# SSD decay exponents from cumulative sums sent through DRAM as rows, and halo copies on ScalarE

## The chip, the core and the metric

The kernel runs on one NeuronCore of a Trainium2 chip. The metric is the device time of one execution in microseconds. Before the change the median of three runs is 3411.99 us (3408.57 to 3416.47).

## The reference, cut to what matters

One hybrid encoder layer over two sequences, 2048 and 256 tokens of width 1024, which the kernel lays out as 18 tiles of 128 tokens. RMSNorm, one input projection, multi-head latent attention beside a bidirectional Mamba-2 (SSD) mixer, an output projection, a SwiGLU FFN and a last RMSNorm. The change touches the SSD mixer alone: for each chunk of 128 tokens, each of 8 heads and each direction it needs the matrix of decays

```
a_cs   = cumsum(dt * a)                  # within a chunk of 128, per head
decay  = exp(where(l >= s, a_cs[l] - a_cs[s], -inf))
scores = einsum(C, B) * decay            # then times x * dt
```

The backward direction is the same with the order of the tokens reversed. The kernel needs exp(...) * dt[s] for both directions, adds the two, and multiplies by C.B.

## The kernel before, in words

Everything is in fp32; most products run as three fp32r products of split operands (`mm3`, L112 to L115). No order is written out by hand in the stage that the change touches: a planner orders each engine's instructions from its own costs, in the order of the program where several are ready, and each engine then runs its list in that order. All transfers are issued by SP's queue, in one list.

Stage A (to about 325 us) normalizes and transposes x, projects the latents, queries, keys, values, gates and dt. Its first transfers are x, `w_a`, one piece of `w_z`, then the small constants (`later`, L76), then cosines (L207), x of the next block (L184) and the rest of `w_z`, `w_kv`, `w_q` (L174). The transposed, split x goes to DRAM as `d_hT`, 2 MB for each block of two tiles.

Stage B (about 325 to 747 us) is the SSD mixer. It first turns dt into softplus(dt) (`dts`) and dt * a (`dsplit`), L386 to L411. `decay_sums` (L571) gets all cumulative sums for the states by small matmuls. Then nine blocks of two tiles pass through a software pipeline, the loop at L582: in step b the block b is projected (`proj`, L436: 192 matmuls of 256 columns, whose result goes by ScalarE at L445 into `X`, three buffers), its two halo columns are copied from and to its neighbour (`halo`, L455 and L456 on GpSimd), block b-1 goes through the five-tap convolution (`conv`: the first tap on ScalarE at L467, four on VectorE at L469, SiLU at L471; `Y`, two buffers), and the two chunks of block b-2 are scanned (`turn`, `scan`). In each half step `decays` (L480) makes the matrix `e` of one chunk. The input of block b+1 (`hT`, two buffers, 2 MB) is loaded at L427 when the block two before it has been projected; blocks 0 and 1 are still in SBUF from stage A.

`decays` before: for each direction GpSimd writes three masked copies of 128 x 1024 (L488): the high and the low part of dt * a and dt itself, each column broadcast over 128 tokens and set to zero on one side of the diagonal. Two pairs of fp32r matmuls (L505, L506) with a mask of ones sum the first two along the partitions, which gives the exponents; ScalarE takes exp from PSUM (L507), VectorE multiplies by the masked dt (L508), adds the directions (L510) and, in `scan`, multiplies by C.B (L538).

After stage B attention starts, whose first products also use L113 to L115.

Of the kernel before, what the change touches and what calls it, by code (L numbers as in the profile page):

```python
# [11 lines left out]
F32 = mybir.dt.float32  # L12
# [8 lines left out]
P = 128  # L21
# [13 lines left out]
WA = QL + KVL + ROPE + 2 * SH  # L35
SCALE = QKD ** -0.5
MAGIC = float(0x5F3759DF)


@with_exitstack  # L40
def hymba_kernel(ctx: ExitStack, tc: tile.TileContext, io, seqs, dbg=None):
# [50 lines left out]
    cmr = const.tile([P, 2, P], F32R, name="cmr")  # L92
    later.append(lambda: nc.vector.tensor_copy(cmr[:, 0, :], m_gt))
    later.append(lambda: nc.vector.tensor_copy(cmr[:, 1, :], m_lt))

    dtall = const.tile([P, NT, 16], F32, name="dtall")

# [3 lines left out]
    d_kr = dram.tile([ROPE, 2, T], F32, name="d_kr")  # L101
    d_v = dram.tile([T, NH, P], F32, name="d_v")
    d_z, d_y, d_C, d_sb = ([dram.tile([P, SW if m != "C" else NG * P], F32, name=f"d_{m}{i}") for i in range(NT)] for m in ("z", "y", "C", "sb"))
    d_x2 = [dram.tile([P, D], F32, name=f"d_x2{i}") for i in range(NT)]

    def f(t):
# [258 lines left out]


    dpool = pool(mixer, "decays", 1)
    dfs, dtd, dec, dts, dah, dal = (dpool.tile([P, 2, NT, SH], F32, name=m) for m in ("dfs", "dtd", "dec", "dts", "dah", "dal"))
    dsplit = dpool.tile([P, 2, NT, SH], F32, name="dsplit")

    with ExitStack() as ph:
# [5 lines left out]
        with ExitStack() as inner:  # L377
            sb = pool(inner, "t_sb", 1)

            def tmp(name):  # L380
                return sb.tile([P, NT, 16], F32, name=name)

            def bc(row):
                return row.rearrange("p (o h) -> p o h", o=1).to_broadcast([P, NT, 16])

            av = sb.tile([P, 16], F32, name="av")  # L386
            nc.scalar.activation(av, alog, AF.Exp)
            nc.vector.tensor_scalar(av, av, -1.0, None, op0=ALU.mult)
# [16 lines left out]
            dhr = sb.tile([P, 2, NT, SH], F32R, name="dhr")  # L405
# [3 lines left out]
            nc.vector.tensor_copy(dhr, dsplit)  # L409
            nc.vector.tensor_copy(dah, f(dhr))  # L410
            nc.vector.tensor_tensor(dal, dsplit, dah, op=ALU.subtract)  # L411

        wp2 = pool(ph, "b_w2", 1)
        wx += [wp2.tile([P, 2, KD, P], F32R, name=f"wx{j}") for j in range(4, KD)]
# [35 lines left out]
        def halo(b, j):  # L450
            c = slice(j, j + 2)
            if bl[b][0] in starts:
                nc.gpsimd.memset(X[b][:, c, 0:2], 0.0)
            else:
                nc.gpsimd.tensor_copy(X[b][:, c, 0:2], X[b - 1][:, c, n:n + 2])  # L455
                nc.gpsimd.tensor_copy(X[b - 1][:, c, n + 2:n + 4], X[b][:, c, 2:4])  # L456
            if last(b):
                nc.gpsimd.memset(X[b][:, c, n + 2:n + 4], 0.0)

# [17 lines left out]
        def hb(a, d, c):  # L477
            return a[:, d, c, :].rearrange("p (h o) -> p h o", o=1).to_broadcast([P, SH, SP])

        def decays(c, even):  # L480

            w = []
            for d in range(2):
                sign = 1 - 2 * d

                def masked(dst, a):

                    nc.gpsimd.affine_select(dst, a[:, d, c, :].rearrange("p (h o) -> p h o", o=1).to_broadcast([P, SH, P]), pattern=[[0, SH], [sign, P]], compare_op=ALU.is_ge, fill=0.0, base=0, channel_multiplier=-sign)  # L488

                rh = mp.tile([P, SH, P], F32R, name="rh", tag="rh")  # L490
                rl = sb.tile([P, SH, P], F32R, name="rl", tag="rl", bufs=1)
                dm = sb.tile([P, SH, P], F32, name="dm", tag="dm", bufs=1)
                masked(rh, dah)
                masked(rl, dal)
                masked(dm, dts)
                if d:
                    e = sb.tile([P, SH, P], F32, name="e1", tag="e1", bufs=1)
                elif even:
                    e = sb.tile([P, SH, P], F32, name="e0", tag="e0", bufs=2)
                else:  # L500
                    e = st.tile([P, SH, P], F32, name="e0", tag="rawx")
                for hh in range(2):
                    s = slice(hh * 4, hh * 4 + 4)
                    pd = bank("ta").rearrange("p (h l) -> p h l", h=4)
# [66 lines left out]
        def decay_sums():  # L571
            for d, (m1, m2) in enumerate(((m_le, m_gt), (m_ge, m_lt))):
                for m, dst in ((m1, dfs), (m2, dtd), (m_one, dec)):
                    ps = bank("mb")[:, :NT * SH]
                    nc.tensor.matmul(ps, m, dsplit[:, d].rearrange("p c h -> p (c h)"), start=True, stop=True)
                    nc.scalar.activation(dst[:, d], ps.rearrange("p (c h) -> p c h", h=SH), AF.Exp)
                nc.vector.tensor_tensor(dtd[:, d], dtd[:, d], dts[:, d], op=ALU.mult)


        nb = len(bl)  # L580
        decay = {}
        for b in range(nb + 2):  # L582
# [8 lines left out]
            for u in range(4):  # L591
# [593 lines left out]
def layout(inputs):  # L1185
# [36 lines left out]
    out["c_mats"] = np.stack([k == l, k <= l, k > l, k >= l, k < l, k >= 0 * l], axis=1).astype(np.float32)  # L1222
    inv = (np.float32(10000.0) ** (-np.arange(0, ROPE, 2, dtype=np.float32) / np.float32(ROPE))).astype(np.float32)
    ang = np.arange(s, dtype=np.float32)[:, None] * inv[None, :]
    out["c_rope"] = np.stack([np.cos(ang), np.sin(ang)], axis=1).astype(np.float32)
    return {n: np.ascontiguousarray(v) for n, v in out.items()}

# [19 lines left out]
```

## Time and profile before

| | us |
|---|---|
| median of three runs | 3411.99 |
| profiled execution | 3416.36 |
| its span, first to last instruction | 3414.7 |
| TensorE busy over the span | 3244.2 (95%) |
| VectorE busy | 2456.1 (72%) |
| ScalarE busy | 1698.0 (50%) |
| GpSimd busy | 609.4 (18%) |
| mean granted clock of TensorE | 0.974 of full |

Busy shares are means over stages with different limits; what the change is worth is read from 325 to 747 us. An instruction's time in the profile holds the time for which it was held up while running. PE is TensorE, DVE VectorE, ACT ScalarE, POOL GpSimd, SP the queue that issues transfers. L numbers are lines of the kernel before.

### The profile page before, as it was taken

What the parts mean: (1) busy time and instruction counts of PE and PEld (TensorE: products, weight loads), DVE (VectorE), ACT (ScalarE), POOL (GpSimd) and SP (SyncE); (2) the same over time, 40 slices, a digit from 0 to 9 for tenths busy, and PEclk for the clock granted to TensorE, in tenths of its full rate; (3) what the DMA queues carried; (4) which work ended last, traced back from release to release, by engine and by line L of the source; (5) the groups of instructions that cost most, each with busy time, mean ns of one, the idle gap of its engine ahead of it and who ended that gap; (6) DMA issues with size and microseconds to landing.
All of it is one profiled execution on the core that took longest, in us unless ns stands there. A gap on an engine that the chain in (4) does not pass through costs nothing.

```text
span 3414.7 us, 48534 instructions
## 1 busy us (share of the span) xinstructions
PE 3244.2 (95%) x17817; PEld 2882.8 (84%) x17817; DVE 2456.1 (72%) x4396; ACT 1698.0 (50%) x3518; POOL 609.4 (18%) x597
## 2 busy tenths in 40 slices
PE   8998999879999999999799799999999999999988
PEld 7897988858888888887688699999999998778777
DVE  6445799978888888887854777787778776354566
ACT  5453444437777777777311545455544444222233
POOL 2222577750000000000310000000000000432630
PEclk9999999979999999999899899999999999999999
DMA  6565222231022111200642333333333333755664
GB/s 253 191 227 186 90 81 75 69 83 37 27 54 52 39 40 41 54 17 15 224 139 99 142 115 122 142 118 118 137 141 132 113 119 118 230 185 172 224 212 137
DMA packets 259166, 407.24 MB, mean 119 GB/s; under 512 B 21424, under 2 KB 170608, under 8 KB 256368
## 3 DMA queue, kind: packets, MB, share of 16 engines
q1 hardware_dynamic: 258928, 404.15, 35.5%
q8 instruction: 140, 2.29, 0.3%
q14 instruction: 98, 0.80, 0.1%
HBM read 274.98 MB, written 129.11 MB: 118 GB/s over the span
## 4 chain that ended last, share of the span: by engine, by line
PE 78%; DVE 11%; DMA 3%; POOL 3%; issue 3%; ACT 2%; SPq 0%; POOLq 0%; ACTq 0%; DVEq 0%
PE bank_mb L1005 8%; PE bank_ma L1005 8%; PE bank_ta L1005 8%; PE bank_ma L113 6%; PE bank_ma L115 6%; PE bank_ma L114 6%; PE bank_mb L113 5%; PE bank_mb L115 5%; PE bank_mb L114 5%; DVE Y L469 4%; PE bank_ta L721 4%; PE bank_o L729 3%; PE bank_o L730 3%; DMA rawd<-w_down 2%; PE bank_tb L721 2%
## 5 line engine op out<-in xcount | busy, mean ns | idle before, releaser
L938 DVE TENSOR_TENSOR ws<-rawf,ws 128x512 fp32r<-128x512 f32 x396 | 267.8, 687 | 97.2 <-ACT ws L937 95.3
L937 ACT ACTIVATE ws<-rawf 128x512 fp32r<-128x512 f32 x396 | 241.8, 627 | 171.7 <-PE bank_ta L1005 37.2
L1005 PE MATMUL bank_ma<-U,ws 128*128 128x384 f32 x1584 | 302.8, 338 | 6.4 <-ACT U L937 3.2
L1005 PE MATMUL bank_mb<-U,ws 128*128 128x384 f32 x1584 | 304.2, 336 | 2.8 <-ACT c L1014 2.5
L1005 PE MATMUL bank_ta<-U,ws 128*128 128x384 f32 x1584 | 297.3, 334 | 3.5 <-ACT U L937 3.0
L1005 PEld LDWEIGHTS bank_ma<-U,ws 128*128 128x128 f32 x1584 | 279.0, 190 | 8.0 <-ACT U L937 3.5
L129 DVE TENSOR_TENSOR pT<-bank_ta,pT 128x512 fp32r<-128x512 f32 (+1 forms) x352 | 239.6, 681 | 63.2 <-ACT pT L128 54.6
L1005 PEld LDWEIGHTS bank_mb<-U,ws 128*128 128x128 f32 x1584 | 277.4, 189 | 5.1 <-ACT c L1014 4.1
L1005 PEld LDWEIGHTS bank_ta<-U,ws 128*128 128x128 f32 x1584 | 276.7, 188 | 4.5 <-ACT U L937 3.3
L128 ACT ACTIVATE pT<-bank_ta 128x512 fp32r<-128x512 f32 (+1 forms) x352 | 209.1, 595 | 116.7 <-PE bank_ta L721 116.2
L1118 POOL TENSOR_TENSOR rawd<-rawd 128x512 f32<-128x512 f32 x33 | 51.5, 1559 | 1189.0 <-DMA rawd<-w_down 1188.6
L729 PE MATMUL bank_o<-pT,v 128*128 128x512 f32 x528 | 248.7, 471 | 1.9 <-ACT ot L736 1.9
L469 DVE SCALAR_TENSOR_TENSOR Y<-X,cw,Y 128x256 f32<-128x256 f32 x288 | 218.5, 815 | 22.9 <-POOL X L456 15.4
L679 DVE TENSOR_REDUCE mx<-bank_ma 128x1 f32<-128x512 f32 (+1 forms) x261 | 177.0, 678 | 50.1 <-PE bank_ma L115 49.5
L721 PE MATMUL bank_ta<-ident,pr 128*128 128x128 f32 x1388 | 210.6, 273 | 2.0 <-DVE pT L129 2.0
L721 PEld LDWEIGHTS bank_ta<-ident,pr 128*128 128x128 f32 x1388 | 170.5, 140 | 48.7 <-DVE pT L129 8.0
L730 PE MATMUL bank_o<-pT,v 128*128 128x512 f32 x528 | 206.2, 391 | 0.0
L1134 ACT ACTIVATE as<-rawa 128x1408 fp32r<-128x1408 f32 x63 | 86.7, 1378 | 225.6 <-PE bank_ma L115 108.6
L688 ACT ACTIVATE pr<-bank_mb,mx 128x512 f32<-128x512 f32 (+1 forms) x261 | 181.4, 695 | 7.9 <-DVE mx L679 4.8
L688 ACT ACTIVATE pr<-bank_ma,mx 128x512 f32<-128x512 f32 (+1 forms) x261 | 179.1, 686 | 6.4 <-DVE mx L707 5.5
L679 DVE TENSOR_REDUCE mx<-bank_mb 128x1 f32<-128x512 f32 (+1 forms) x261 | 176.9, 678 | 7.0 <-PE bank_mb L115 3.7
L752 POOL TENSOR_TENSOR mla<-lo,ri 128x256 f32<-128x256 f32 (+1 forms) x40 | 22.8, 570 | 855.6 <-DVE lo L751 842.5
(399 smaller groups left out, 8584.9 us busy)
## 6 DMA issues: line engine op xcount, KB each, us to landing
rawf<-w_gu SPq DMA_DIRECT2D x66, 1024.0 KB, 5.8
rawa<-d_A SPq DMA_DIRECT2D x63, 704.0 KB, 5.2
rawd<-w_down SPq DMA_DIRECT2D x154, 256.0 KB, 4.9
d_A<-c SPq DMA_DIRECT2D x132, 192.0 KB, 1.9
d_A<-s SPq DMA_DIRECT2D x99, 192.0 KB, 1.9
o<-d_x SPq DMA_DIRECT2D x32, 512.0 KB, 4.8
d_hT<-hT SPq DMA_DIRECT2D x7, 2048.0 KB, 12.9
hT<-d_hT SPq DMA_DIRECT2D x7, 2048.0 KB, 7.9
```

Source lines behind the costliest of these rows:

```text
L113: nc.tensor.matmul(ps, wh, xh, start=start, stop=False)
L114: nc.tensor.matmul(ps, wh, xl, start=False, stop=False)
L115: nc.tensor.matmul(ps, wl, xh, start=False, stop=stop)
L469: nc.vector.scalar_tensor_tensor(y[:, j, :], x[:, j, t:t + n], cw[:, j, t:t + 1], y[:, j, :], op0=ALU.mult, op1=ALU.add)
L679: nc.vector.tensor_reduce(mx[:, j:j + 1], ps[:, :m * P], axis=AX.X, op=ALU.max, negate=nch == 1)
L688: nc.scalar.activation(e[:, :m * P], ps[:, :m * P], AF.Exp, bias=bias, accum_out=rs[:, i, j:j + 1])
L721: nc.tensor.transpose(ps[:, i * P:(i + 1) * P], pr[i, kt // 4][:, kt % 4 * P:(kt % 4 + 1) * P], ident)
L729: nc.tensor.matmul(po[0][:, :n], v[:, s0 + kt, :], pT[:, 0, :n], start=kt == 0, stop=False)
L730: nc.tensor.matmul(po[0][:, :n], v[:, s0 + kt, :], pT[:, 1, :n], start=False, stop=kt == sn - 1)
L937: nc.scalar.activation(dst[:, 0], src, AF.Copy)
L938: nc.vector.tensor_tensor(dst[:, 1], src, f(dst)[:, 0], op=ALU.subtract)
L1005: nc.tensor.matmul(ps[:, :W], w[:, a, k, :], x[:, b, k, :], start=k + n == 0 and not more, stop=k == HK - 1 and n == 2, skip_group_check=more)
```

## The change: what it does

The masked copies go. Instead the exponents of all chunks are made once and sent through DRAM as rows, and each chunk loads its rows.

Once, at the end of step 0: dt * a is split on a fixed grid into `coarse` and `fine`, `off` is ln(dt); `decay_sums` takes the cumulative sums of `coarse` and `fine` by four more small matmuls, and `off` becomes ln(dt) minus the fine sum. `cum_rows` transposes the three arrays (nine transposes), splits each into two fp32r parts (tile `part`, which shares the two buffers of `Y`) and writes them to `d_cum` and `d_off` with 144 transfers, all on SP. `d_cum` holds a block-diagonal arrangement whose other entries must be zero, so the whole of it, 36 x 32768 numbers (4.72 MB), is copied from an input of zeros beforehand, as the last of the constants in `later`.

For each chunk: `load_rows`, eight transfers (four for each direction), fills the rows 0-15, 16-31 of two halves of `r` (64 x 1024) and `o` (64 x 128); the other rows are constants. There is one `r` and one `o` for each direction, loaded for chunk c+1 after the products of chunk c. `decays` then is, for each half, one fp32r product of `o` and `r` with 64 rows, which gives the difference of cumulative sums plus ln(dt), and one of the identity with a mask of -2^100, and exp. The product by the masked dt (L508) is gone.

The two halo copies go from GpSimd to ScalarE.

```diff
+    later.append(lambda: nc.sync.dma_start(d_cum.rearrange("g a q x -> g (a q x)"), io["c_zero"]))
...
+            nc.vector.tensor_scalar(coarse, dsplit, GRID, None, op0=ALU.add)
+            nc.vector.tensor_scalar(coarse, coarse, -GRID, None, op0=ALU.add)
+            nc.vector.tensor_tensor(fine, dsplit, coarse, op=ALU.subtract)
+            nc.vector.tensor_scalar(off, dts, 1e-37, None, op0=ALU.max)
+            nc.scalar.activation(off, off, AF.Ln)
...
-                nc.gpsimd.tensor_copy(X[b][:, c, 0:2], X[b - 1][:, c, n:n + 2])
-                nc.gpsimd.tensor_copy(X[b - 1][:, c, n + 2:n + 4], X[b][:, c, 2:4])
+                nc.scalar.activation(X[b][:, c, 0:2], X[b - 1][:, c, n:n + 2], AF.Copy)
+                nc.scalar.activation(X[b - 1][:, c, n + 2:n + 4], X[b][:, c, 2:4], AF.Copy)
...
+        def load_rows(c):
+            for d in range(2):
+                r, o = fix[d]
+                for a in range(2):
+                    nc.sync.dma_start(f(r)[a * 32:a * 32 + 16], d_cum[d * NT + c, a].rearrange("q (h x) -> (q h) x", h=SH).rearrange("k (h l) -> k h l", h=SH))
+                    nc.sync.dma_start(f(o)[a * 32 + 16:a * 32 + 32], d_off[d * NT + c, a].rearrange("q h l -> (q h) l"))
...
-                masked(rh, dah)
-                masked(rl, dal)
-                masked(dm, dts)
...
-                    nc.tensor.matmul(pd, cmr[:, d, :], rh[:, s, :], start=True, stop=False)
-                    nc.tensor.matmul(pd, cmr[:, d, :], rl[:, s, :], start=False, stop=True)
+                    nc.tensor.matmul(pd, o, r[:, s, :], start=True, stop=False)
+                    nc.tensor.matmul(pd, identr, never[:, d:d + 1, :].to_broadcast([P, 4, P]), start=False, stop=True)
                     nc.scalar.activation(e[:, s, :], pd, AF.Exp)
-                nc.vector.tensor_tensor(e, e, dm, op=ALU.mult)
...
+        def cum_rows():
+            G3 = 12
+            for src, a, to in ((coarse, 0, "both"), (fine, 1, "cum"), (off, 1, "off")):
+                flat = src.rearrange("p d c h -> p (d c h)")
+                ps = bank("mb")[:96, :384]
+                for t in range(3):
+                    nc.tensor.transpose(ps[:, t * P:(t + 1) * P], flat[:, t * 96:(t + 1) * 96], ident)
+                part = sb.tile([96, 2, 3, P], F32R, name="part", tag="Y")
+                flatp = part.rearrange("p q t l -> p q (t l)")
+                nc.scalar.activation(flatp[:, 0], ps, AF.Copy)
+                nc.vector.tensor_tensor(flatp[:, 1], ps, f(flatp)[:, 0], op=ALU.subtract)
+                n, w = SH - 1, (SH + 1) * P
+                for g in range(G3):
+                    p = f(part)[g * SH:(g + 1) * SH]
+                    for q in range(2):
+                        if to != "cum":
+                            nc.sync.dma_start(d_off[g::G3, a, q].rearrange("t h l -> h t l"), p[:, q])
+                        if to != "off":
+                            nc.sync.dma_start(d_cum[g::G3, a, q, :n * w].rearrange("t (h x) -> h t x", h=n)[:, :, :P], p[:n, q])
+                            nc.sync.dma_start(d_cum[g::G3, a, q, n * w:].rearrange("t (h x) -> h t x", h=1), p[n:, q])
...
+                for t in (coarse, fine):
+                    ps = bank("mb")[:, :NT * SH]
+                    nc.tensor.matmul(ps, m1, t[:, d].rearrange("p c h -> p (c h)"), start=True, stop=True)
+                    nc.vector.tensor_copy(t[:, d], ps.rearrange("p (c h) -> p c h", h=SH))
+                nc.vector.tensor_tensor(off[:, d], off[:, d], fine[:, d], op=ALU.subtract)
+            cum_rows()
+            load_rows(bl[0][0])
...
                     decay[c] = decays(c, b % 2 == 0)
+                    if c + 1 < NT:
+                        load_rows(c + 1)
```

## Rows read from the trace of the kernel before

**Rows 1.** The page's part 2: busy tenths of VectorE and GpSimd in 40 equal slices of the span (85.4 us each).

```profile
DVE  6445799978888888887854777787778776354566
POOL 2222577750000000000310000000000000432630
```

**Rows 2.** Busy time by stretch: a steady block of the SSD loop, and the stage's end (columns: the stretch, its length, then busy us with the count of instructions for PE, PEld, DVE, ACT and POOL, granted clock, DMA share, GB/s).

```profile
449.00:493.50 44.50, 39.84 (x286) 37.34 (x285) 41.09 (x47) 18.53 (x30) 33.47 (x31) 0.96 0.21 78
...
670.00:745.00 75.00, 56.62 (x276) 46.64 (x275) 61.55 (x61) 24.61 (x41) 55.80 (x41) 0.77 0.29 79
```

**Rows 3.** What TensorE waited for from 449 to 493.5 us (us in total, times, the longest).

```profile
PE bank_o L567 <- DVE e L538: 3.2, 2, 2.5
PE bank_tb L554 <- DVE ns L558: 1.5, 1, 1.5
```

**Rows 4.** VectorE's groups from 325 to 745 us, shapes kept apart (busy us, mean ns, idle before and its releasers).

```profile
L469 DVE SCALAR_TENSOR_TENSOR Y<-X,cw,Y 128x256 f32<-128x256 f32 x288 | 218.5, 815 | 22.9 <-POOL X L456 15.4 <-ACT Y L467 7.2
L508 DVE TENSOR_TENSOR e<-e,dm 128x1024 f32<-128x1024 f32 x36 | 60.9, 1691 | 14.5 <-ACT e L507 6.5 <-POOL dm L488 4.3 <-POOL rh L488 3.7
L538 DVE TENSOR_TENSOR e<-e,bt 128x1024 f32<-128x1024 f32 x18 | 29.8, 1654 | 0.1
L510 DVE TENSOR_TENSOR e<-e,e 128x1024 f32<-128x1024 f32 x18 | 27.6, 1533 | 0.3
L568 DVE TENSOR_TENSOR yo<-bank_o,yo 128x512 f32<-128x512 f32 x18 | 12.2, 679 | 2.2 <-PE bank_o L567 2.2
```

**Rows 5.** The tile X: the convolution's taps on VectorE (ns, min/median/max).

```profile
L469 DVE SCALAR_TENSOR_TENSOR Y<-X,cw,Y x288: 468/476/1511, 334.4 to 710.4; 128x256 f32<-128x256 f32 x144
```

**Rows 6.** GpSimd's groups from 325 to 745 us.

```profile
L488 POOL TENSOR_SCALAR_AFFINE_SELECT rh<-dah 128x1024 fp32r<-128x1024 f32 x36 | 52.9, 1470 | 38.7 <-PE bank_ta L505 38.7
L488 POOL TENSOR_SCALAR_AFFINE_SELECT rl<-dal 128x1024 fp32r<-128x1024 f32 x36 | 51.3, 1424 | 0.0
L531 POOL TENSOR_TENSOR xd<-xs,dtd 128x512 f32<-128x512 f32 x36 | 49.9, 1401 | 5.5 <-PE bank_tb L554 5.2 <-POOL ns L557 0.4
L488 POOL TENSOR_SCALAR_AFFINE_SELECT dm<-dts 128x1024 f32<-128x1024 f32 x36 | 47.5, 1320 | 31.4 <-DVE e L508 31.4
L557 POOL TENSOR_TENSOR ns<-ns,dec 128x512 f32<-128x512 f32 x16 | 23.4, 1463 | 8.4 <-DVE ns L558 8.4
L527 POOL TENSOR_TENSOR yo<-xs,rows 128x512 f32<-128x512 f32 x18 | 22.4, 1245 | 1.0 <-ACT xs L518 1.0
L549 POOL TENSOR_TENSOR yo<-yo,to 128x512 f32<-128x512 f32 x16 | 22.0, 1374 | 18.3 <-DVE to L548 18.3
```

**Rows 7.** ScalarE in order of time: evictions of projected block pairs (start us, us). The four evictions of a block end its projection; 372.56 is block 1's last, 677.29 is block 8's last.

```profile
372.56 0.60 ACT L445 ACTIVATE X<-bank_ma 128x512 f32<-128x512 f32 x1 [3.91 <-PE bank_ma L115]
...
677.29 0.60 ACT L445 ACTIVATE X<-bank_ma 128x512 f32<-128x512 f32 x1 [5.10 <-PE bank_ma L115]
```

**Rows 8.** The chain of waits: stage A's last store, and attention's first product.

```profile
324.18 6.31 DMA d_v<-vs
...
747.33 0.79 PE bank_tb L113
```

**Rows 9.** What VectorE waited for from 670 to 750 us (us in total, times, the longest).

```profile
DVE to L548 <- PE bank_tb L546: 6.7, 2, 4.7
...
DVE yo L568 <- PE bank_o L567: 2.2, 1, 2.2
DVE ns L558 <- PE bank_tb L554: 1.4, 1, 1.4
```

**Rows 10.** SP's time for the issue of one transfer (ns, min/median/max): C by head group and queries, which have three levels of addresses, and the plain store of y.

```profile
L473 SPq DMA_DIRECT2D d_C<-Y x18: 518/584/628, 382.1 to 714.2; - x18
L299 SPq DMA_DIRECT2D d_q<-kq x40: 550/584/3165, 66.8 to 321.9; - x40
L569 SPq DMA_DIRECT2D d_y<-yo x18: 319/322/401, 399.8 to 745.2; - x18
```

**Rows 11.** Transfers from 300 to 760 us: median us from issue to landing.

```profile
hT<-d_hT SPq DMA_DIRECT2D x7, 2048.0 KB, 7.9
...
d_q<-kq SPq DMA_DIRECT2D x8, 384.0 KB, 6.4
...
d_C<-Y SPq DMA_DIRECT2D x18, 128.0 KB, 2.2
```

**Rows 12.** The page's part 6: stores of hT over the whole run.

```profile
d_hT<-hT SPq DMA_DIRECT2D x7, 2048.0 KB, 12.9
```

**Rows 13.** SP in order of time at the start: the last constant, the next x, the rest of w_z.

```profile
11.65 0.33 SPq L76 DMA_DIRECT2D rows<-c_rows  x1
...
14.18 1.86 SPq L184 DMA_DIRECT2D xt<-x  x4
...
16.64 2.56 SPq L174 DMA_DIRECT2D raw<-w_z  x3
```

**Rows 14.** What SP's queue waited for in the first 60 us: four of the constants each for one of the four transfers of w_a, issued eight before them.

```profile
SPq L76 <- DMA raw<-w_a: 3.5, 4, 1.0
```

**Rows 15.** TensorE in order of time in stage A: the last gate product of the first block, the first query product.

```profile
37.73 0.39 PE L115 MATMUL bank_mb<-wz,hT 128*128 128x512 f32 x1
...
41.87 0.66 PE L113 MATMUL bank_ma<-wq,lT 128*128 128x384 f32 x1 [0.33 <-ACT lT L131]
```

**Rows 16.** SP in order of time: the loads of blocks 2 and 3 (two transfers, with the wait between them).

```profile
348.86 24.02 SPq L427 DMA_DIRECT2D hT<-d_hT  x2
```

More of the change, by code (lines that the diff above doesn't have):

```diff
@@ L37 @@
 MAGIC = float(0x5F3759DF)
+GRID = 1.5 * 2.0 ** 13
 @with_exitstack
@@ L91, in hymba_kernel @@
     dtb, alog, dskip = rows[:, 0:16], rows[:, 16:32], rows[:, 32:40]
-    cmr = const.tile([P, 2, P], F32R, name="cmr")
-    later.append(lambda: nc.vector.tensor_copy(cmr[:, 0, :], m_gt))
-    later.append(lambda: nc.vector.tensor_copy(cmr[:, 1, :], m_lt))
+    identr = const.tile([P, P], F32R, name="identr")
+    later.append(lambda: nc.vector.tensor_copy(identr, ident))
+    never = const.tile([P, 2, P], F32R, name="never")
+    for d, m in enumerate((m_gt, m_lt)):
+        later.append(lambda d=d, m=m: nc.vector.tensor_scalar(never[:, d], m, -2.0 ** 100, None, op0=ALU.mult))
     dtall = const.tile([P, NT, 16], F32, name="dtall")
@@ L103, in hymba_kernel @@
     d_z, d_y, d_C, d_sb = ([dram.tile([P, SW if m != "C" else NG * P], F32, name=f"d_{m}{i}") for i in range(NT)] for m in ("z", "y", "C", "sb"))
+    d_cum = dram.tile([2 * NT, 2, 2, SH * SH * P], F32, name="d_cum")
+    d_off = dram.tile([2 * NT, 2, 2, SH, P], F32, name="d_off")
+    later.append(lambda: nc.sync.dma_start(d_cum.rearrange("g a q x -> g (a q x)"), io["c_zero"]))
     d_x2 = [dram.tile([P, D], F32, name=f"d_x2{i}") for i in range(NT)]
@@ L367, in hymba_kernel @@
     dpool = pool(mixer, "decays", 1)
-    dfs, dtd, dec, dts, dah, dal = (dpool.tile([P, 2, NT, SH], F32, name=m) for m in ("dfs", "dtd", "dec", "dts", "dah", "dal"))
+    dfs, dtd, dec, dts, coarse, fine, off = (dpool.tile([P, 2, NT, SH], F32, name=m) for m in ("dfs", "dtd", "dec", "dts", "coarse", "fine", "off"))
     dsplit = dpool.tile([P, 2, NT, SH], F32, name="dsplit")
@@ L404, in hymba_kernel @@
             nc.vector.tensor_tensor(da, u, bc(av), op=ALU.mult)
-            dhr = sb.tile([P, 2, NT, SH], F32R, name="dhr")
             for d in range(2):
@@ L408, in hymba_kernel @@
                 nc.vector.tensor_copy(dsplit[:, d], da[:, :, d * SH:(d + 1) * SH])
-            nc.vector.tensor_copy(dhr, dsplit)
-            nc.vector.tensor_copy(dah, f(dhr))
-            nc.vector.tensor_tensor(dal, dsplit, dah, op=ALU.subtract)
+            nc.vector.tensor_scalar(coarse, dsplit, GRID, None, op0=ALU.add)
[3 more added lines that the diff above has]
+            nc.scalar.activation(off, off, AF.Ln)
         wp2 = pool(ph, "b_w2", 1)
@@ L478, in hb @@
             return a[:, d, c, :].rearrange("p (h o) -> p h o", o=1).to_broadcast([P, SH, SP])
+        fix = {}
+        for d in range(2):
+            r = mp.tile([64, SH, P], F32R, name=f"rows{d}")
+            o = mp.tile([64, P], F32R, name=f"offs{d}")
+            raw = sb.tile([64, SH + 1, P], F32, name="rk", tag="Y")
+            nc.sync.dma_start(raw, io["c_rk"].rearrange("k (h l) -> k h l", l=P))
+            nc.vector.tensor_copy(o, raw[:, 0])
+            nc.vector.tensor_copy(r, raw[:, 1:])
+            fix[d] = r, o
+        def load_rows(c):
+            for d in range(2):
+                r, o = fix[d]
+                for a in range(2):
+                    nc.sync.dma_start(f(r)[a * 32:a * 32 + 16], d_cum[d * NT + c, a].rearrange("q (h x) -> (q h) x", h=SH).rearrange("k (h l) -> k h l", h=SH))
+                    nc.sync.dma_start(f(o)[a * 32 + 16:a * 32 + 32], d_off[d * NT + c, a].rearrange("q h l -> (q h) l"))
         def decays(c, even):
@@ L483, in decays @@
             for d in range(2):
[L484 to L492, printed above, removed]
-                masked(rh, dah)
-                masked(rl, dal)
-                masked(dm, dts)
+                r, o = fix[d]
                 if d:
@@ L1224, in layout @@
     ang = np.arange(s, dtype=np.float32)[:, None] * inv[None, :]
+    rk = np.zeros((2, 2, 2, SH, P + SH * P), np.float32)
+    rk[:, 0, :, :, :P] = 1.0
+    rk[:, 1, :, :, P:] = np.repeat(np.eye(SH), P, axis=1)
+    rk[0, 1] *= -1.0
+    rk = rk.reshape(64, -1)
+    out["c_rk"] = rk
+    out["c_zero"] = np.zeros((2 * (a["x_prompt"].shape[1] + a["x_sample"].shape[1]) // P, 4 * SH * SH * P), np.float32)
     out["c_rope"] = np.stack([np.cos(ang), np.sin(ang)], axis=1).astype(np.float32)
```

## The prediction, made before the change was run

> **What bounds the kernel now.** I read the page's slices first: in slices 5 to 9 VectorE is at eight to nine tenths and GpSimd at five to seven, more than anywhere else [rows 1]. Then the stretches: in a steady block of the SSD loop, 44.5 us, VectorE is busy 41.1 and TensorE 39.8 [rows 2]. TensorE's waits there, 4.7 us, all name VectorE [rows 3], so VectorE ends last. Its groups say why: the 288 taps of the convolution take 815 ns in the mean [rows 4] but 476 in the median [rows 5], and the large products 1533 to 1691. Taps run beside GpSimd's masked copies and wait for them inside their own time; L568, which reads PSUM, stays at 679. The stage ends 70.0 us after block 8's last eviction: 677.3 to 747.3 [rows 7, 8], a tail in which VectorE is busy 61.6 of 75 us and TensorE's clock is granted at 0.77 [rows 2].
>
> **The change part by part.**
>
> **1. The steady loop.** GpSimd loses 52.9 + 51.3 + 47.5 = 151.7 us of masked copies and keeps 49.9 + 23.4 + 22.4 + 22.0 = 117.7 [rows 6], 44% of the 269. VectorE loses L508, 60.9 us. I scale what the taps lose to GpSimd (815 - 476 = 339 ns) by that 44%: 149, so a tap takes about 625 ns. For a block: 32 x 0.625 = 20.0; L538 and L510 at 1.4 us each (between 0.97, the taps' ratio of 476 to 815, and their mean of 1.65), twice each, 5.6; six operations from PSUM at 0.68, 4.1. Sum 29.7 against 41.1 now, so VectorE no longer ends last.
> TensorE is late next. Its matmuls stay equal in number and columns (four of 512 columns for each direction, of which half now have 64 rows; the extra ones come once). What it needs for a block: 44.5 less 4.7 of waits, less 4% for the clock at 0.96 [rows 2, 3] (1.8 us): 38.0. I take 39.0 with one us of waits left; the bounds are 38.0 and 42.0 (half the gain kept). Blocks 2 to 8 took 677.3 - 372.6 = 304.7 us [rows 7]; 7 x 39 = 273. **Gain 31.7** (11 to 39).
> The halo copies on ScalarE: it is busy 18.5 of 44.5 us [rows 2]; eight copies of four columns per block cost at most 8 x 0.6, the price of a whole eviction [rows 7], and lie beside its idle time. VectorE's 15.4 us of waits for L456 [rows 4] lie in the gain above. Below nothing: the copy follows the eviction on the same engine.
> `load_rows`, 16 transfers per block at 0.32 to 0.58 us [rows 10], 7 us of SP, and 2 to 3 us to land [rows 11]: they start when chunk c's products have read `r` and have half a block, 20 us, until the next. Queued behind them on SP are d_y, d_C and hT, none needed within 7 us. I cost it at nothing; if they come late each time, a few us per chunk (rival D).
>
> **2. The tail.** L508 goes, and VectorE's backlog of taps with it. What it must do after the last eviction: 8 taps at 0.625 and four scans at 2.8 + 2.0: 24 us; its waits for TensorE's chain stay, 6.7 + 2.2 + 1.4 [rows 9]. That is 35; I take 38. **Gain 32** (20, if 20 us of taps are still behind, to 37).
>
> **3. The burst on SP.** The 144 transfers: coarse 12 x 2 x 3 = 72, fine 48, off 24. Of them 48 take one partition and go at d_y's 0.32 us, 96 have three levels as d_C and queries, 0.58 [rows 10]: 15 + 56 = 71 us of issue. They start at about 337: the space comes free when d_v lands at 330.5 [rows 8], then tables, sums, transposes and splits. The first 120 are ready together and end at about 395, the rest and load_rows(0) at 412. The load of block 2's input stands at 348.9 now [rows 16], when block 0 has been projected; it comes later in the program, so it queues behind 120 to 152 transfers: issued 395 to 412, landed 7.9 us later [rows 11], 403 to 420. TensorE, which now ends block 1 at 372.6 and goes on, has nothing else to run there: the scans need the same rows, and the first convolution a buffer of `Y` that `part` holds until its transfers have landed (395). So block 2 begins at 412 in place of 373. **Loss 39.** Bounds: 19, if the planner puts the hT load in front (then three blocks are projected by 396 and the first rows still land at about 415); 85, if each transfer costs 0.8 us (rival B).
>
> **4. The zero fill.** 4.72 MB, issued behind the last constant at 12 us, ahead of x, w_z, w_kv and w_q [rows 13]. At hT's rate, 2.1 MB in 7.9 us [rows 11], it takes 18 us; at the store's 12.9 us [rows 12], 29. What comes after it is late by that: the queue seems to allow eight transfers outstanding (each of four constants waited for the w_a piece eight before it [rows 14]), so the third w_z piece and all after it wait for its landing. TensorE now ends the first gates at 37.7 and starts on the queries at 41.9 [rows 15]. With the last w_z pieces 18 us later it ends them near 53 and the queries start there: **loss 12** (0, if the planner puts it past the loads; 23 at the slower rate). TensorE is full until 300, so nothing gives it back.
> The rate of a copy from DRAM to DRAM stands in no row. The Trainium skill, page "DMA: Bandwidth & Descriptors", section "Why a DMA increments its semaphore by 16 and not by 1", says that such a transfer runs on the largest number of engines up to 16 that divides its slowest dimension on both sides; 36 rows would make that 12, the fill 18 x 16/12 = 24 us, and the sum about 6 us worse. No run here shows it.
>
> **5. Small things.** Ln on ScalarE, two table loads and the coarse, fine and off arithmetic lie ahead of the burst and are in its 337. The tables `never` and `identr` replace `cmr`, three copies for two.
>
> **The sum.** -31.7 - 32 + 39 + 12 = -12.7. The profiled execution took 3416.4 us, 4.4 above the median: 3403.7 in its terms, 3399 against the median of 3412.0.
>
> **The rivals.**
> **B, slower: the burst lasts.** Each of the 144 waits for a slot among eight outstanding, and stores land in 6.4 us as those of the queries do in this stretch [rows 11]: 6.4 / 8 = 0.8 us each. The hT load then stands behind 120 x 0.8 = 96 us: 337 + 96 + 8 = 441, a loss of 68. Sum -63.7 + 68 + 12 = +16: 3428. It decides once a transfer costs more than 0.65 us (gain 63.7 - 12 = 52 us used up). For it: a list that no one overtakes, DRAM stores of 512-byte pieces, and in-order ScalarE and VectorE lists planned as if they landed sooner. Against: d_C and d_y land in about 2 us.
> **C, faster by much: the burst is out of the way.** The planner puts the hT loads ahead, or an issue costs 0.32 throughout (46 us, to 383, block 2 at 391): a loss of 19, and a fill at nothing to 12. Sum -63.7 + 19 + 6 = -39: 3373. For it: SP is idle most of the stage. Against: the order of the program.
> **D, slower: rows late in every chunk.** One `r` per direction, so TensorE's list stands still if SP is held by a store at its head. Three us in 18 chunks, 54, in place of the loop's gain: sum near +25, 3437. SP's list waited for y, but the rows have 20 us.
> **How the numbers follow.** The forecast 0.45, C 0.20, B 0.25, D 0.10. Within the forecast, sd about 12 us: faster by over 0.2% (7 us, about what a measurement of this kernel can tell from no change) 0.29 of the 0.45, within 0.13, slower 0.03; C all faster; B and D 0.31 slower and 0.04 within. Faster 0.49, same 0.17, slower 0.34. The range takes in C and B and part of D: 3365 to 3438; the forecast's own is 3384 to 3414.
>
> **What would show it.** In the profile after: taps near 0.6 us and no L488 (1); evictions of a block 39 us apart and TensorE's waits for VectorE gone; attention's first product some 38 us after block 8's last eviction (2); 144 short issues on SP from about 337 in a row, the second hT load behind them, TensorE without work between about 373 and 412 (3); w_z landing near 44 us and the first query product near 53 (4). Wrong: taps still at 0.8; TensorE waiting for `r` in each step; block 2 projected before 395, or not until after 430.

## The result, and the profile after

The changed kernel takes 3438.62 us (3438.19 to 3439.08), the kernel before in the same session 3410.28: a ratio of 1.008, 95% interval 1.0063 to 1.0098. It is slower by some 28 us where 13 us faster was forecast.

Both traces can be cut at the same events. First ScalarE's list in the kernel before (start us, us): the first eviction of the SSD stage, block 2's first, and the stage's last operation; [rows 7] has block 1's last and block 8's last.

```profile
329.38 0.59 ACT L445 ACTIVATE X<-bank_ma 128x512 f32<-128x512 f32 x1
...
384.39 0.61 ACT L445 ACTIVATE X<-bank_ma 128x512 f32<-128x512 f32 x1
...
746.68 0.60 ACT L560 ACTIVATE ns<-bank_tb 128x512 f32<-128x512 f32 x1 [6.87 <-PE bank_tb L554]
```

The same five events in the changed kernel, where the eviction is L456 and the state copy L599:

```profile
344.31 0.59 ACT L456 ACTIVATE X<-bank_ma 128x512 f32<-128x512 f32 x1
...
383.71 0.60 ACT L456 ACTIVATE X<-bank_ma 128x512 f32<-128x512 f32 x1 [4.82 <-PE bank_ma L124]
...
447.54 0.60 ACT L456 ACTIVATE X<-bank_ma 128x512 f32<-128x512 f32 x1 [4.32 <-PE bank_ma L124]
...
716.54 0.60 ACT L456 ACTIVATE X<-bank_ma 128x512 f32<-128x512 f32 x1 [5.15 <-PE bank_ma L124]
...
770.21 0.60 ACT L599 ACTIVATE ns<-bank_tb 128x512 f32<-128x512 f32 x1 [5.28 <-PE bank_tb L593]
```

| stretch | before, us | after, us | difference |
|---|---|---|---|
| start to the stage's first eviction | 329.4 | 344.3 | +14.9 |
| to block 1's last eviction | 43.2 | 39.4 | -3.8 |
| to block 2's first eviction | 11.8 | 63.8 | +52.0 |
| to block 8's last eviction | 292.9 | 269.0 | -23.9 |
| to the stage's last operation | 69.4 | 53.7 | -15.7 |
| the rest of the span | 2668.0 | 2666.0 | -2.0 |

The differences add up to +21.5, which is that of the two spans (3436.2 less 3414.7). It is less than 28 because the profiled execution of the kernel before took 3416.36 us, 6 more than the median. Each stretch has its own view.

**The start.** SP in order of time, then what SP's queue waited for from 12 to 45 us, then what TensorE waited for in the first 60 us of the changed kernel (us in total, times, the longest):

```profile
12.97 0.63 SPq L112 DMA_DIRECT2D d_cum<-c_zero  x1
...
29.57 0.33 SPq L216 DMA_DIRECT2D cs<-c_rope  x1
30.01 1.45 SPq L183 DMA_DIRECT2D raw<-w_z  x2
```

```profile
SPq L216 <- DMA d_cum<-c_zero: 12.3, 1, 12.3
```

```profile
PE bank_ta L206 <- DMA raw<-w_z: 12.3, 1, 12.3
```

The eighth transfer behind the fill waits for the fill, and the rest of `w_z` behind that; TensorE's first query product comes at 54.2 us (41.9 in [rows 15]).

**The burst.** SP's first transfer of the burst, its last eleven with the load behind them; then TensorE's longest wait from 345 to 470 us:

```profile
348.56 0.34 SPq L547 DMA_DIRECT2D d_off<-part  x1
...
418.88 3.81 SPq L547 DMA_DIRECT2D d_off<-part  x11
...
426.44 0.37 SPq L438 DMA_DIRECT2D hT<-d_hT  x1
```

```profile
PE bank_ta L523 <- DMA offs<-d_off: 42.3, 1, 42.3
```

The 144 transfers go out back to back for 74 us; the load of block 2's input, at 348.86 us in [rows 16], stands behind all of them and the first eight row loads. ScalarE's list stands too: the first tap of the next convolution waits 28 us for a `Y` slot that `part` holds until its transfers have landed.

```profile
415.33 4.04 ACT L478 ACTIVATE Y<-X,cb,cw 128x256 f32<-128x256 f32 x8 [28.15 <-DMA d_cum<-part]
```

**A steady block.** Busy time in one block from first eviction to first eviction (columns as in [rows 2]), and VectorE's taps over the stage, which answer to [rows 4]:

```profile
492.86:533.53 40.67, 40.67 (x285) 36.66 (x284) 28.90 (x42) 19.52 (x38) 11.83 (x10) 1.00 0.29 100
```

```profile
L480 DVE SCALAR_TENSOR_TENSOR Y<-X,cw,Y 128x256 f32<-128x256 f32 x288 | 166.3, 642 | 59.8 <-ACT X L467 31.4 <-ACT Y L478 28.5
```

VectorE fell from 41.1 to 28.9 us a block, as the forecast had it (29.7). But TensorE is busy the whole 40.67 us and waits for nothing; the forecast gave it 38.0. The reason stands in TensorE's list (start us, us):

```profile
556.34 0.50 PE L523 MATMUL bank_ta<-rows,offs 64*128 64x512 f32 x1
556.77 0.50 PE L524 MATMUL bank_ta<-never,identr 128*128 128x512 f32 x1
557.20 0.49 PE L523 MATMUL bank_ta<-rows,offs 64*128 64x512 f32 x1
557.62 0.50 PE L524 MATMUL bank_ta<-never,identr 128*128 128x512 f32 x1
```

Products of 512 columns at full clock follow each other 0.43 us apart here. They alternate between 64 and 128 rows, which none of the kernel before's decay products did.

**The tail.** Busy time in the last stretch, its first two pieces and the sum over all three:

```profile
716.50:732.50 16.00, 14.18 (x70) 9.97 (x69) 14.83 (x23) 10.61 (x20) 9.14 (x6) 1.00 0.67 158
732.50:752.00 19.50, 19.36 (x58) 12.93 (x59) 13.26 (x21) 7.26 (x9) 5.77 (x4) 0.56 0.10 32
...
sum 53.70, PE 49.04 PEld 35.43 DVE 36.09 ACT 21.95 POOL 26.26; mean PE 16.35 PEld 11.81 DVE 12.03 ACT 7.32 POOL 8.75
```

VectorE is busy 36.1 us, where the forecast's 38 held 24 us of its work and waits for the rest. TensorE is busy 49.0 of 53.7 us, 19.4 of them at a mean granted clock of 0.56, which is mostly the lower of its two levels (1.2 GHz); it fell there after a piece at full clock in which TensorE was busy 14.2 of 16.0 us.

### The profile page after: what moved, and what is told of

It reads as the page before. It is cut to its first block, busy times and chain, and to the rows that moved or that the text cites. A ratio compares the mean times of both kernels' runs of the same rounds, so it can differ in the third digit from the quotient of the medians.

```text
span 3436.2 us, 48810 instructions
## 1 busy us (share of the span) xinstructions
PE 3261.7 (95%) x17834; PEld 2882.3 (84%) x17834; DVE 2343.7 (68%) x4375; ACT 1712.8 (50%) x3580; POOL 425.9 (12%) x433
## 4 chain that ended last, share of the span: by engine, by line
PE 86%; DVE 5%; DMA 2%; ACT 2%; SPq 2%; issue 1%; POOL 1%; POOLq 0%; ACTq 0%; DVEq 0%
PE bank_mb L1053 8%; PE bank_ma L1053 8%; PE bank_ta L1053 8%; PE bank_ma L122 7%; PE bank_ma L124 7%; PE bank_ma L123 7%; PE bank_mb L122 6%; PE bank_mb L124 5%; PE bank_mb L123 5%; PE bank_ta L769 4%; PE bank_o L777 3%; PE bank_o L778 3%; PE bank_tb L769 2%; PE bank_o L1053 2%; PE bank_tb L1053 2%
## 5 line engine op out<-in xcount | busy, mean ns | idle before, releaser
L480 DVE SCALAR_TENSOR_TENSOR Y<-X,cw,Y 128x256 f32<-128x256 f32 x288 | 166.3, 642 | 59.8 <-ACT X L467 31.4
L124 PE MATMUL bank_ma<-hT,wx 128*128 128x256 f32 x576 | 164.8, 286 | 2.7 <-DVE wx L133 2.7
```

Of the source, the lines that this page charges most:

```text
L124: nc.tensor.matmul(ps, wl, xh, start=False, stop=stop)
```

## The experiments

My theory after this reading: three costs lie one behind the other on TensorE's list, the fill (some 14 us), the burst (some 50) and the alternation of row counts (3 us a block). The rivals are in the expectations. Ratios are to the kernel before, run on the same chip; what an edit gains on the changed kernel is the difference of two such ratios, each with its interval.

### The fill, moved and by itself

The first kernel has the fill in the first stage, in its third block; the second is the kernel before with one line more.

```diff
+            if b == 2:
+                nc.sync.dma_start(d_cum[0:1, 0, 0, :8], lats[0][0:1, :8])
+                nc.sync.dma_start(d_cum.rearrange("g a q x -> g (a q x)"), io["c_zero"])
```

```diff
+    later.append(lambda: nc.sync.dma_start(d_cum.rearrange("g a q x -> g (a q x)"), io["c_zero"]))
```

> The same kernel with the zero fill of d_cum issued in the middle of the first stage (behind the first tile of its third block, by a small transfer that it must wait for) in place of 13 us; nothing is left out. Theory: the fill delays the start by what the first eviction of the SSD stage is late, 14.9 us (344.3 against 329.4), and nothing gives it back: first query product near 42 us again, first eviction of the SSD stage near 330, time 3424 (3420 to 3428). Rival 1, the delay was given back before the end of the stage or is another edit's: 3436 to 3441. Rival 2, the fill costs as much wherever it stands, because it takes the DMA engines from the loads of x: 3434 to 3440, with TensorE waiting for x in the third block.

Measured: 3425.69 us, ratio 1.0045 (1.0032 to 1.0057), against 1.008: some 12 us less. The first query product is at 41.6 us, the stage's first eviction at 330.5, and TensorE waits for nothing from 100 to 200 us, where the fill now is. Rival 2 falls.

> The kernel before with the zero fill alone added, at its place behind the constants; nothing else reads d_cum. Theory: plus 12 to 15 us, 3422 to 3426, first query product near 54 us as in the changed kernel. Rival, the fill is hidden or given back: within 4 us of the kernel before, 3406 to 3414.

Measured: 3422.54 us, ratio 1.004 (1.0027 to 1.0052), some 14 us more than before, with the same wait in SP's queue:

```profile
SPq L209 <- DMA d_cum<-c_zero: 13.1, 1, 13.1
```

So the fill costs 12 to 14 us at its place, and next to nothing 130 us later.

### The rows of the decay products

The first kernel has 128 rows in both products, the second 64 in both.

```diff
-            r = mp.tile([64, SH, P], F32R, name=f"rows{d}")
-            o = mp.tile([64, P], F32R, name=f"offs{d}")
-            raw = sb.tile([64, SH + 1, P], F32, name="rk", tag="Y")
+            r = mp.tile([P, SH, P], F32R, name=f"rows{d}")
+            o = mp.tile([P, P], F32R, name=f"offs{d}")
+            raw = sb.tile([P, SH + 1, P], F32, name="rk", tag="Y")
+            nc.gpsimd.memset(raw, 0.0)
```

```diff
-                    nc.tensor.matmul(pd, identr, never[:, d:d + 1, :].to_broadcast([P, 4, P]), start=False, stop=True)
-                    nc.scalar.activation(e[:, s, :], pd, AF.Exp)
+                    nc.tensor.matmul(pd, identr[:64], never[:64, d:d + 1, :].to_broadcast([64, 4, P]), start=False, stop=True)
+                    nc.scalar.activation(e[:, s, :], pd, AF.Exp, scale=0.0)
```

> The changed kernel with the operands r and o of the decay products 128 partitions high, rows 64 to 127 zero: every product of a decay has 128 rows, the result is the same. Theory: the decay products follow each other in 0.43 us in place of 0.235 because a weight load of another number of rows doesn't run beside the matmul before it; 16 per block give 3.1 us. Back at 0.235 us the steady block is 37.6 to 38.5 us in place of 40.7, seven blocks give 15 to 22 us, the tail some 2 to 5: 3413 to 3421. Rival, the 0.43 us come from the operands (a broadcast view of never, float32 bits in DRAM) or from TensorE's load in general: block 40.7, time 3436 to 3441.

Measured: 3419.54 us, ratio 1.0028 (1.0019 to 1.0037), 18 us less than the changed kernel. TensorE's list with 128 rows throughout, and a steady block:

```profile
548.74 0.40 PE L525 MATMUL bank_ta<-never,identr 128*128 128x512 f32 x1
548.97 0.40 PE L524 MATMUL bank_ta<-rows,offs 128*128 128x512 f32 x1
549.21 0.40 PE L525 MATMUL bank_ta<-never,identr 128*128 128x512 f32 x1
```

```profile
489.58:527.23 37.65, 37.65 (x285) 36.30 (x284) 28.85 (x42) 19.14 (x38) 12.79 (x10) 1.00 0.32 108
```

More rows, all zero, make the products faster: 0.23 to 0.24 us apart, and 37.65 us a block. The tail stays: 52.6 us.

The weight loads of the same products (PEld, start us, us) show what is lost, in the changed kernel and then with 128 rows throughout:

```profile
556.77 0.19 PEld L524 LDWEIGHTS bank_ta<-never,identr 128*128 128x128 f32 x1 [0.24 <-issue]
557.20 0.18 PEld L523 LDWEIGHTS bank_ta<-rows,offs 64*128 64x128 f32 x1 [0.25 <-issue]
```

```profile
548.74 0.19 PEld L524 LDWEIGHTS bank_ta<-rows,offs 128*128 128x128 f32 x1
548.97 0.19 PEld L525 LDWEIGHTS bank_ta<-never,identr 128*128 128x128 f32 x1
```

With mixed rows a load starts together with its own product (556.77, 557.20). With 128 rows it starts with the product ahead, 0.23 us before its own (548.74 for the product at 548.97). So the load does not run beside the product ahead where the number of rows changes, as the theory had it.

> The changed kernel with the mask product on 64 rows too (identr and never cut to their first 64 partitions), and the exponential taken with scale 0: left out are half of the mask and the decays' values; the instructions are equal in number. Theory: what stops a weight load from running beside the matmul ahead of it is the change of the number of rows; two products of 64 rows after each other then start about 0.235 us apart, rows to never, and the steady block is 38.5 to 40 us (the first and last product of each series still change the number). Rival: a product of 64 rows lets no load run beside it whatever follows: 0.43 us from start to start as in the changed kernel, block 40.7.

Measured, in a single execution: 3431.91 us. What counts here are its products of 64 rows behind each other, and a block:

```profile
553.69 0.49 PE L523 MATMUL bank_ta<-rows,offs 64*128 64x512 f32 x1
554.03 0.39 PE L524 MATMUL bank_ta<-never,identr 64*128 64x512 f32 x1
554.27 0.39 PE L523 MATMUL bank_ta<-rows,offs 64*128 64x512 f32 x1
554.50 0.39 PE L524 MATMUL bank_ta<-never,identr 64*128 64x512 f32 x1
554.83 0.39 PE L122 MATMUL bank_ma<-hT,wx 128*128 128x256 f32 x1
```

```profile
531.26:571.16 39.90, 39.90 (x285) 36.19 (x284) 28.82 (x42) 19.41 (x38) 11.91 (x10) 1.00 0.29 101
```

From the second product of the four on the distance is 0.23 to 0.24 us again. It is 0.34 us from the first to the second and 0.33 from the last to the next product of 128 rows, that is, next to a change of the number of rows. The rival, a product of 64 rows as such, falls. Counting settles it: in TensorE's list the eight products of a chunk stand as one run of four and two pairs. In the changed kernel that is 8 changes of the number of rows per chunk, 16 per block: (40.67 - 37.65) / 16 = 0.19 us each. With 64 rows in both it is 2 + 2 + 2 = 6 per chunk, 12 per block: (39.90 - 37.65) / 12 = 0.19.

### The burst: which of its effects holds TensorE

In the first kernel `d_cum` and `d_off` are indexed [a, q, chunk] and a chunk of `d_cum` is padded to SH * (SH + 1) * P, so that one transfer takes the 96 rows of all groups:

```diff
-                for g in range(G3):
-                    p = f(part)[g * SH:(g + 1) * SH]
-                    for q in range(2):
...
+                for q in range(2):
+                    p = f(part)[:, q]
+                    if to != "cum":
+                        nc.sync.dma_start(d_off[a, q].rearrange("(t g) h l -> (g h) t l", t=3), p)
+                    if to != "off":
+                        nc.sync.dma_start(d_cum[a, q].rearrange("(t g) (h x) -> (g h) t x", t=3, h=SH)[:, :, :P], p)
```

The second moves the load, the third the buffers, the fourth does both with the 144 transfers left as they are:

```diff
             if b == 0:
+                load_h(2)
                 decay_sums()
```

```diff
-                part = sb.tile([96, 2, 3, P], F32R, name="part", tag="Y")
+                part = sb.tile([96, 2, 3, P], F32R, name="part", tag="e1" if src is off else "e0", bufs=1 if src is off else 2)
```

> The changed kernel with d_cum's chunks padded to SH + 1 rows, so that the 96 rows of a third lie at one stride in DRAM: 8 transfers write the rows in place of 144; load_rows takes 16 transfers per chunk in place of 8 (one for each q); the fill is larger by an eighth. Theory: it was the 74 us of issue on SP that held the load of block 2's input; that load now goes at about 355, block 2's first eviction is near 395 in place of 447.5, TensorE's wait of 42 us for the first rows is under 10, time 3385 to 3398. Rival, the rows are late by their own chain (tables, transposes, splits through the two Y slots), whatever the number of transfers: the wait keeps 20 us or more and the time is 3412 to 3430. Second rival: 16 small loads per chunk come late in each chunk: PE waits for rows in the steady blocks, over 41 us per block.

Measured: 3388.41 us, ratio 0.993 (0.9917 to 0.9944): 51 us less than the changed kernel and faster than the kernel before. Five of the eight transfers go out in 3.1 us, the others by 358 us, and TensorE's one wait from 345 to 470 us is for a weight split:

```profile
349.81 0.33 SPq L547 DMA_DIRECT2D d_off<-part  x1
350.19 0.46 SPq L549 DMA_DIRECT2D d_cum<-part  x1
350.69 0.48 SPq L547 DMA_DIRECT2D d_off<-part  x1
351.22 1.67 SPq L549 DMA_DIRECT2D d_cum<-part  x2
```

```profile
PE bank_ma L124 <- DVE wx L133: 1.8, 1, 1.8
```

Both rivals fall: the tables and transposes make nothing late, and 16 small loads per chunk leave the block at 40.67 us. A transfer of 96 partitions with three pieces each costs SP 0.33 to 0.48 us in the first three rows, no more than one of the 144.

> The changed kernel with load_h(2) called ahead of decay_sums, so that the load of block 2's input stands behind 45 of the 144 transfers in SP's list and not behind 152; nothing else is changed. Theory: the burst holds TensorE in two ways, by this load and by the first rows. With the load at about 372 us block 2 is projected from 384 to 410 or so, and only then does TensorE wait for the rows, until about 427: of the 42 us of the wait 20 to 30 go, 3438.6 becomes 3409 to 3419. Rival: the first rows alone decide (or the Y slots that part holds until the burst has landed), the projections of block 2 only fill a wait that ends at the same time and the work behind it is as late as before: 3432 to 3441.

Measured: 3428.34 us, ratio 1.0043 (1.003 to 1.0057), 13 us less: between the theory (20 to 30) and the rival (none). TensorE's wait for the rows fell from 42.3 to 26.1 us, but new waits came behind it:

```profile
PE bank_ta L523 <- DMA offs<-d_off: 26.1, 1, 26.1
PE bank_tb L593 <- POOL xd L570: 4.6, 1, 4.6
```

ScalarE's list still stood before the first tap, until 420.47 us, for a `Y` slot. So the load is one hold among several.

> The changed kernel with part, the tile that the 144 transfers read, in buffers of e0 and e1 (not used before the first decay) in place of those of Y; nothing else is changed. Theory: the burst holds TensorE in three places (the load of block 2's input, the first rows, the two Y slots that the first convolutions need). With the Y slots free the convolutions of blocks 0 and 1 are done before 400 us and not from 415 on, but the load and the rows still come at 426: 5 to 15 us less than the changed kernel, 3424 to 3434. Rival: the Y slots alone held it: over 25 us less, below 3414.

Measured: 3431.59 us, ratio 1.0056 (1.0042 to 1.007), 8 us less, within the theory's range, though this interval and the changed kernel's (1.0063 to 1.0098) overlap: the slots' own share is barely clear of nothing.

> Both edits, part in buffers of its own and load_h(2) ahead of decay_sums; the burst of 144 transfers stays. Theory: block 2 is projected and blocks 0 and 1 are convolved while the burst runs, and at 428 us only the decays are left to do: TensorE waits from 410 to 428 and has a block's projections done by then, 25 to 35 us less than the changed kernel, 3404 to 3414. Rival: the first rows at 427 alone set when the loop goes on, and what was done ahead is lost again by the three buffers of X: as with the load alone, 3424 to 3432.

Measured: 3414.5 us, ratio 1.0006 (0.9997 to 1.0015), 25 us less, the least that the theory gave, at a time just outside its range (3404 to 3414). TensorE's wait for the rows:

```profile
PE bank_ta L523 <- DMA offs<-d_off: 10.5, 1, 10.5
```

With the load and the slots out of the way half of the burst's 51 us goes. The other half goes with the 8 transfers, which also bring the rows early; that it is the rows' share follows by subtraction, since no run has the rows early and the rest unchanged.

### The halo copies

The kernel before with this part of the change alone (and, further down, the best kernel without it):

```diff
-                nc.gpsimd.tensor_copy(X[b][:, c, 0:2], X[b - 1][:, c, n:n + 2])
-                nc.gpsimd.tensor_copy(X[b - 1][:, c, n + 2:n + 4], X[b][:, c, 2:4])
+                nc.scalar.activation(X[b][:, c, 0:2], X[b - 1][:, c, n:n + 2], AF.Copy)
+                nc.scalar.activation(X[b - 1][:, c, n + 2:n + 4], X[b][:, c, 2:4], AF.Copy)
```

> The kernel before with the halo copies on ScalarE and nothing else of the change. Theory: the copies cost ScalarE nothing that is on the path, and VectorE's waits for GpSimd's copies (15.4 us in the stage, of which part is the wait for the eviction itself) go: 3396 to 3408. Rival 1: the waits were for the eviction, not for the copy: 3406 to 3414. Rival 2: eight more instructions per block in ScalarE's list put evictions and exponentials behind the copies' waits: over 3414.

Measured: 3413.61 us, ratio 1.0001 (0.9992 to 1.0009). The theory is wrong. The time lies at the upper end of rival 1 and 0.4 us under rival 2's, and the trace shows something of both. VectorE still waits 11.4 us in the stage ahead of its taps, now for ScalarE's copy, where it waited 15.4 for GpSimd's. Its waits for ScalarE's exponentials rose from 6.5 us to 32.7 [rows 4 has both before], as rival 2 said. What was gained at the copies was then, as I read it, lost again at the exponentials; no run takes the two apart.

```profile
L469 DVE SCALAR_TENSOR_TENSOR Y<-X,cw,Y 128x256 f32<-128x256 f32 x288 | 207.2, 779 | 13.8 <-ACT X L456 11.4 <-ACT Y L467 2.5
L508 DVE TENSOR_TENSOR e<-e,dm 128x1024 f32<-128x1024 f32 x36 | 56.6, 1572 | 35.7 <-ACT e L507 32.7 <-POOL dm L488 3.0
```

### The three mended together

The 8 transfers, the late fill and the 128 rows in one kernel, whose edits are those shown above.

> The changed kernel with the 8 merged transfers, the fill in the middle of the first stage and the operands of 128 rows together. Theory: the three costs lie one after the other on TensorE's list, so that their gains add: 1.008 less 0.015 (8 transfers), 0.0035 (fill) and 0.0052 (128 rows) of the kernel before, 0.984: 3356, 3350 to 3364. Rival: with TensorE's block at 37.6 us another engine or the 16 row loads end last, and half of the gain of the 128 rows is lost: 3364 to 3375.

Measured: 3353.47 us (3352.46 to 3356.03), ratio 0.9826 (0.9813 to 0.9839): 60 us below the 3413.75 of the kernel before in that session, and 0.0254 below the changed kernel's 1.008. The three single gains add to 0.015 + 0.0035 + 0.0052 = 0.0237. A steady block:

```profile
424.42:462.07 37.65, 37.65 (x285) 36.30 (x284) 28.84 (x42) 19.14 (x38) 12.81 (x10) 1.00 0.31 107
```

> The kernel with 8 transfers, the late fill and 128 rows, with the halo copies back on GpSimd: tells what this part of the change is worth where TensorE is never waited for. Theory: nothing, within 4 us of the kernel with them on ScalarE, a ratio to the kernel before of 0.9815 to 0.984. Rival: GpSimd's copies come late behind its own list and the taps wait for them: 1 us per block and more, a ratio over 0.985.

Measured: 3351.0 us (3349.01 to 3352.4), ratio 0.9817 (0.9804 to 0.983), the same as with the copies on ScalarE within the intervals, as expected. This version, with the halo copies left on GpSimd, is as fast as any that was run.

## Why the prediction was wrong, by its steps

The forecast's sum was -12.7; the trace's is +21.5, 34 apart. By the table the tail is 16 us worse than forecast, the burst 13, the loop 8 and the fill 3; two stretches that the forecast left out give 6 back.

**Step 1, the steady loop: wrong in one sentence.** "Its matmuls stay equal in number and columns", and so 38.0 us a block. The number and the columns did stay equal; the row counts did not, and I had named them in the bracket behind ("half now have 64 rows") without pricing them. Sixteen changes of 0.19 us made 40.67. Without them the block is 37.65, below the 38.0 that I took for a floor and the 39.0 I chose. The Trainium skill's page "TensorE: Matmul & The Clock Gate", section "Step-by-step: what each phase is for", says that the timing goes by columns and the number of rows doesn't matter, and that the next weights are loaded ahead when the row groups don't conflict or the load goes to a background buffer. For products of one number of rows the runs agree (0.23 to 0.24 us with 64 and with 128); where the number changes they don't. The rest of the step held: taps 0.642 us (0.625 forecast), VectorE 28.9 (29.7), no waits for `load_rows`, halo copies at nothing (both runs).

**Step 2, the tail: wrong, and the largest miss.** 38 us forecast, 53.7 measured. The sum counted 8 taps behind block 8's last eviction. There are 32, all of that block's, and the trace of before already had them. VectorE's taps from the last eviction to the stage's end, first before, then after, and its longest waits after:

```profile
L469 DVE SCALAR_TENSOR_TENSOR Y<-X,cw,Y 128x256 f32<-128x256 f32 x32 | 27.2, 907 | 0.0
```

```profile
L480 DVE SCALAR_TENSOR_TENSOR Y<-X,cw,Y 128x256 f32<-128x256 f32 x32 | 19.3, 659 | 0.3 <-ACT Y L478 0.3
L587 DVE TENSOR_TENSOR to<-bank_tb,dfs 128x512 f32<-128x512 f32 x4 | 2.8, 690 | 14.4 <-PE bank_tb L585 14.4
```

The taps take 19.3 us in place of 5.0, which brings VectorE's work to 36.1 in place of 24. It sits idle for the other 17.6 us, in place of the 10.3 of waits that the sum carried over from before. These two terms make up the miss: 12 + 7, less the 3 added in taking 38 for 35. VectorE's part and TensorE's also lie one behind the other: to 732.6 us the chain that ended last runs mostly over VectorE, behind that mostly over TensorE, which is busy 49.0 us in the whole tail. Mixed rows and the low clock are not what makes it long: with 128 rows throughout and granted clocks of 0.87, 0.76 and 0.95 in its three pieces the tail is 52.6 us with TensorE busy 43.8. What the tail would be with the taps done earlier no run shows.

**Step 3, the burst: right mechanism, too small.** The issue took 74 us (71 forecast), and the load stood behind it. The loss was 52 in place of 39. I put block 2's start at 412, the load's issue being between 395 and 412 and its landing 8 us later; in fact the load stood behind all 152 transfers. Subtracting the fill's delay of 12 from 426.4 gives 414, the late end, and its landing is at 422, ten later than I took. The rows came at the same time and the `Y` slots were free only at 415. The runs with the load and the slots out of the way gave 13 and 8 us back one by one and 25 together; the rest of the 51 is put down to the rows. The parts were also distributed otherwise: the one-partition transfers, which I priced at 0.32 us, are the dearest. That 71 came so near 74 is in part luck: by the medians below, the 48 of one partition took 32 us in place of 15 and the other 96 took 31 in place of 56, and the gaps between issues make up the rest. The bound of 85 and rival B's 68 also priced the same 0.8 us twice, once for all 144 transfers and once for 120.

The rows of the three kinds, with one, eight and seven partitions, in the view of each line (ns, min/median/max):

```profile
L550 SPq DMA_DIRECT2D d_cum<-part x48: 662/662/797, 349.3 to 413.5; - x48
...
L547 SPq DMA_DIRECT2D d_off<-part x48: 264/350/449, 348.6 to 422.4; - x48
...
L549 SPq DMA_DIRECT2D d_cum<-part x48: 273/294/442, 348.9 to 413.0; - x48
```

**Step 4, the fill: right.** 12 forecast, 12 (moved) to 14 (alone) by the runs, 14.9 at the stage's first eviction. The transfer eight behind it was issued 16.6 us after the fill (29.57 less 12.97), which fits the 18 us taken from hT's rate. My estimate by the rule of the Trainium skill's page "DMA: Bandwidth & Descriptors", section "Why a DMA increments its semaphore by 16 and not by 1", was 12 engines for 36 rows and 24 us; the trace does not bear that out here. From 14.5 to 27 us, while only the fill's packets moved, the DMA view (packets, MB, their time as a share of 16 engines) has all 16 engines' time filled, and in the trace's packet records 16 packets are under way at once:

```profile
q1 hardware_dynamic: 88, 4.33, 102.3%
```

Which dimension the instruction carried, and so what the rule would have given, no view shows.

**The rivals.** B named the right place, but not the price: a transfer took 0.51 us of issue (74 / 144), under its point of 0.65, and the loss came all the same. C did not happen; the 8 transfers are C made on purpose. D is false: from 493 to 696 us TensorE waits for nothing. That the measured 3438.6 lies beside D's 3437 is chance; D's +25 does not even follow from its terms, since 54 us on top of the rest of the sum give more. As to the prediction's first paragraph, VectorE's digits in slices 5 to 9 are 7, 9, 9, 9, 7 and not eight to nine; nothing else hangs on that.

## What to carry to other kernels

When an engine is about to become the bound, its own list has to be priced again from the changed instructions (shape, rows, neighbours), not carried over from the trace in which it had slack. What is left to do at the end of a stage can be counted in the trace of before, and should be. Many small transfers in one place cost by their number: look for a layout in DRAM in which their addresses lie at one stride (8 transfers did here what 144 did), and list everything that stands behind the burst, the buffers that its source holds included. A large transfer that nobody needs soon belongs behind the loads that somebody does.

## What the runs showed of the hardware that I had not expected

- A product whose number of rows differs from that of the one before it started late: 0.19 us for each change, worked out two ways above, with products of 512 columns 0.23 to 0.24 us apart otherwise at full clock. Filling up to 128 rows with zeros was faster than the 64 rows that were needed. The weight load then starts with its own product and not with the product ahead of it (both at 556.77, against 548.74 for a product at 548.97 where the rows are equal); why a change of rows brings that about the runs don't show.
- A transfer from one partition (three pieces of 512 bytes) cost SP 0.66 us of issue, one from eight partitions 0.35 and one from seven 0.29 (medians of 48). One partition was the dearest; between seven and eight it was the other way round, and whether the partitions or the layout in DRAM set it was not tested.
